# HGRN scores of a hybrid encoder layer: 128x128 score matmuls against two 64x64 matmuls on the halves of TensorE's columns

## The chip, the cores and the metric

The kernel runs on one core of a Trainium2 chip. The core has a matrix engine (TensorE, PE in the profile, with its weight loads shown apart as PEld), VectorE (DVE), ScalarE (ACT), GpSimd (POOL), SyncE (SP) and 16 DMA engines. TensorE reads both operands from SBUF and writes PSUM; ACT and DVE copy results out of PSUM. The metric is the device time of one execution in microseconds, the median over several runs.

## The reference

One encoder layer over 512 tokens of width 1024. Its first part mixes tokens in four HGRN heads and four mLSTM heads, each 128 wide; a cross-attention and a squared-ReLU MLP follow. The change touches the HGRN heads alone. Each head runs a gated scan forward and backward, and the two are summed:

```
S_t = diag(f_t) S_{t-1} + k_t v_t^T        (k_t = 1 - f_t)
o_t = S_t^T q_t
```

Written out, `o_t` is a sum over tokens `s` of a score times `v_s`, and the score is the sum over the 128 channels of `q_t k_s` times the product of the forget gates between `s` and `t`. That product depends on the channel, so scores can't be one plain matmul.

## The kernel before

Channels lie on the 128 partitions and the 512 tokens on the free axis. All large products are made of three fp32r matmuls (high by high, high by low, low by high: `mm3`, lines 225 to 227), each with 512 moving columns. For each 128x1024 piece of a weight matrix, ACT rounds it into `wh` (line 221) and DVE subtracts to get `wl` (line 222); a pair feeds 24 matmuls.

The HGRN scores are built by levels. For L = 1, 2, 4, ..., 64 the tokens are cut into blocks of 2L, and the scores between the two halves of such a block come from one product of `kc` (keys that are already multiplied by the gates up to the half's edge; made by `kcomb` on ACT, line 366) with the like-prepared queries `q2`. After each level `update` (DVE, lines 426, 429 and 433) multiplies queries, keys and gates by the next stretch of gates. Tokens are taken in four windows of 128, so a level is four fp32 matmuls of 128 keys by 128 tokens into one PSUM tile `sm` (line 376), and a predicated copy on DVE (line 381) takes from it the entries that belong to this level, by the mask `lm`, into the four diagonal blocks of the score matrix `A`. Ahead of the levels, line 361 makes the scores of a token with itself in the same way, and ACT copies them (line 362).

A fp32 matmul stands in the profile as two weight loads and two matmuls ("passes" below), so a score group of four matmuls has eight passes. A head's chain has one group of line 361 and seven of line 376; with four heads there are 32 groups.

The chain is a generator (`hgrn_chain`), and each `yield` gives way to the projections. Two heads are started at a time ("first pair", "second pair"). For the first pair, one step of a chain is taken after every 12 large matmuls; for the second (`rate[0] = 2`) two are taken, so that the groups of both heads stand together. The order on each engine is fixed when the program is built. On TensorE the instructions run in that order.

Of the kernel before, what the change touches and what calls it, by code (L numbers as in the profile page):

```python
# [13 lines left out]
AF = mybir.ActivationFunctionType  # L14
# [4 lines left out]
P = 128  # L19
# [58 lines left out]
def trunk(ctx: ExitStack, tc: tile.TileContext, x, mem, wpk, vec, cst, lmask, rmask, rows, out):  # L78
# [5 lines left out]
    v, sc, gp, pe = nc.vector, nc.scalar, nc.gpsimd, nc.tensor  # L84
    cnt = [0]

    def nm(s):
        cnt[0] += 1
        return f"{s}_{cnt[0]}"
# [7 lines left out]
    def smb():  # L97
        return pss.tile([P, 512], F32, tag="sm", name=nm("sm"))
# [4 lines left out]
    def ap(t, off, *dims):  # L103
        a = t[:, :]
        return bass.AP(a.tensor, a.offset + off, [list(a.ap[0])] + [list(d) for d in dims])
# [14 lines left out]
    lm = sb.tile([P, len(LEVELS) * P], U8, name="lm")  # L120
# [117 lines left out]
    def proj_d(mat, c0, xs, n=512, count=2):  # L238

        for j in range(count):  # L240
            wh, wl = weights(("d", mat, 0, c0 + P * j))
            ps = mmb()
            for k in range(8):
                z = slice(k * P, k * P + P)
                mm3(ps[:, :n], wh[:, z], wl[:, z], xs[k][0], xs[k][1], k == 0, k == 7)
                if k == 3:
                    tick()
            yield ps
            tick()
# [37 lines left out]
    for t in range(4):  # L287
# [4 lines left out]
        with tc.high_priority():  # L292
            for g in range(2):
                xg = xt[:, g * 512:g * 512 + 512]
                v.scalar_tensor_tensor(out=xg, in0=xg, scalar=r, in1=gmix[g], op0=ALU.mult, op1=ALU.mult)
                ps = smb()
# [51 lines left out]
    def hgrn_chain(h, s_):  # L348
        q, f, k = s_["q"], s_["f"], s_["k"]
        q2 = A4()  # L350
        v.tensor_tensor(out=q2[:, 0:512], in0=q[:, 0:512], in1=f[:, 512:1024], op=ALU.mult)
        v.tensor_tensor(out=q2[:, 512:1024], in0=q[:, 0:512], in1=f[:, 0:512], op=ALU.mult)
        A = A16()
        Adiag = ap(A, 0, [512 + P, 4], [1, P])
        kc = T2()
        v.tensor_tensor(out=kc[:, 0:512], in0=k[:, 0:512], in1=k[:, 512:1024], op=ALU.add)
        yield
        ps = smb()
        for w in range(4):
            z = slice(w * P, w * P + P)  # L360
            pe.matmul(ps[:, z], lhsT=kc[:, z], rhs=q[:, z], start=True, stop=True)
        sc.activation(Adiag, ps[:, :].rearrange("p (w t) -> p w t", t=P), AF.Copy)

        def kcomb(L):
            t = T2()
            sc.activation(t[:, 0:512].rearrange("p (b e j) -> p b e j", e=2, j=L),  # L366
                          ap(k, 0, [2 * L, 512 // (2 * L)], [512 + L, 2], [1, L]), AF.Copy)
            return t

        kc = kcomb(1)  # L370
        yield
        for li, L in enumerate(LEVELS):
            ps = smb()
            for w in range(4):
                z = slice(w * P, w * P + P)
                pe.matmul(ps[:, z], lhsT=kc[:, z],  # L376
                          rhs=ap(q2, w * P, [2 * L, P // (2 * L)], [512 + L, 2], [1, L]), start=True, stop=True)
            update(q2, k, f, L)
            if L < 64:
                kc = kcomb(2 * L)  # L380
            v.copy_predicated(Adiag, lm[:, li * P:li * P + P].unsqueeze(1).to_broadcast([P, 4, P]),
                              ps[:, :].rearrange("p (w t) -> p w t", t=P))
            yield

        ps = smb()
        for b in range(2):
            w0, w1 = slice(b * 256, b * 256 + P), slice(b * 256 + P, b * 256 + 256)
            pe.matmul(ps[:, b * 256 + P:b * 256 + 256], lhsT=k[:, w0], rhs=q2[:, 512 + b * 256 + P:512 + b * 256 + 256], start=True, stop=True)
            pe.matmul(ps[:, b * 256:b * 256 + P], lhsT=k[:, 512 + b * 256 + P:512 + b * 256 + 256], rhs=q2[:, w0], start=True, stop=True)

        sc.activation(ap(A, P, [1024 + 256, 2], [1, P]), ap(ps, P, [256, 2], [1, P]), AF.Copy)
        sc.activation(ap(A, 512, [1024 + 256, 2], [1, P]), ap(ps, 0, [256, 2], [1, P]), AF.Copy)
        update(q2, k, f, 128)
        yield

        for dr in range(2):
            ps = smb()
            for i in range(2):
                if dr == 0:
                    pe.matmul(ps[:, i * 256:i * 256 + 256], lhsT=k[:, i * P:i * P + P], rhs=q2[:, 768:1024], start=True, stop=True)  # L400
                else:
                    pe.matmul(ps[:, i * 256:i * 256 + 256], lhsT=k[:, 768 + i * P:768 + i * P + P], rhs=q2[:, 0:256], start=True, stop=True)
            dst = ap(A, 256, [512, 2], [1, 256]) if dr == 0 else ap(A, 1024, [512, 2], [1, 256])
            sc.activation(dst, ps[:, :].rearrange("p (i t) -> p i t", t=256), AF.Copy)
        yield
        ps = smb()
        for t in range(4):
            for s in range(4):
                pe.matmul(ps[:, t * P:t * P + P], lhsT=A[:, s * 512 + t * P:s * 512 + t * P + P],
                          rhs=vh[s][:, h * P:h * P + P], start=(s == 0), stop=(s == 3))  # L410
        o = T2()
        sc.activation(o[:, 0:512], ps, AF.Copy)
        yield
        yield from head_out(o, s_["gate"], V_HN + h, h)

    def update(q2, k, f, L):
        nb = 512 // (2 * L)
        if L == 128:
            qa, ta = ap(q2, 0, [896, 2], [1, P]), ap(f, 640, [-384, 2], [0, P])
            v.tensor_tensor(out=qa, in0=qa, in1=ta, op=ALU.mult)  # L420
            ka, tb = ap(k, 0, [896, 2], [1, P]), ap(f, 128, [640, 2], [0, P])
            v.tensor_tensor(out=ka, in0=ka, in1=tb, op=ALU.mult)
            return
        qa = ap(q2, 0, [512 + L, 2], [2 * L, nb], [1, L])
        ta = ap(f, 512 + L, [-(512 + L), 2], [2 * L, nb], [0, L])
        v.tensor_tensor(out=qa, in0=qa, in1=ta, op=ALU.mult)
        ka = ap(k, 0, [512 + L, 2], [2 * L, nb], [1, L])
        tb = ap(f, L, [512 - L, 2], [2 * L, nb], [0, L])
        v.tensor_tensor(out=ka, in0=ka, in1=tb, op=ALU.mult)
        if L < 128:  # L430
            fa = ap(f, 0, [512, 2], [2 * L, nb])
            fb = ap(f, L, [512, 2], [2 * L, nb])
            v.tensor_tensor(out=fa, in0=fa, in1=fb, op=ALU.mult)

    def head_out(o, gate, gcol, idx):

        junk = T2()
        ss = tiny(4)
        for t in range(4):
            z = slice(t * P, t * P + P)  # L440
            sc.activation(junk[:, z], o[:, z], AF.Square, accum_out=ss[:, t:t + 1])
        r, _ = rstd_of(ss, 4, P)
        v.tensor_tensor(out=o[:, 0:512].rearrange("p (t e) -> p t e", e=P),
                        in0=o[:, 0:512].rearrange("p (t e) -> p t e", e=P),
                        in1=r.unsqueeze(2).to_broadcast([P, 4, P]), op=ALU.mult)
        yield
        ps = smb()
        for t in range(4):
            z = slice(t * P, t * P + P)
            pe.transpose(ps[:, z], o[:, z], ident)  # L450
        v.scalar_tensor_tensor(out=gate, in0=ps, scalar=vc[:, gcol:gcol + 1], in1=gate, op0=ALU.mult, op1=ALU.mult)
        ys[idx] = hl(YT1())
        split_out(ys[idx][0], ys[idx][1], gate)
        yield
# [221 lines left out]
    def hgrn_start(p):  # L676
        for j in range(2):
            chains.append(hgrn_chain(2 * p + j, hst[2 * p + j]))
# [25 lines left out]
    for t in range(2):  # L704
        a = mt[t]
# [14 lines left out]
    for k in range(8):  # L720
        ps = smb()
# [226 lines left out]
    for f in range(4):  # L948

        sta = []  # L950
        for p in range(4):
            a = []
            for j in range(2):
                ps, = proj_d("up", 1024 * f + P * (p + 4 * j), x3, count=1)
# [57 lines left out]
        def ahead(n):  # L1012
            with tc.high_priority():
                for m in range(n, n + 3):
                    job(f, m)
            return job(f, n)

        n = 0
        while n < len(JOBS):
            p, g = JOBS[n]  # L1020
# [8 lines left out]
            w = ahead(n)  # L1029
# [96 lines left out]
```

## Time and profile before

| | before |
|---|---|
| median of 3 runs | 881.77 us (881.75 to 882.56) |
| profiled execution | 882.23 us, its span 880.4 us |
| PE busy, instructions | 855.4 us (97%), 4198 |
| DVE busy | 609.7 us (69%) |
| ACT busy | 415.2 us (47%) |
| granted TensorE clock | 1.00 in every stretch of the HGRN part |

A busy share says how long an engine had work under way. In the long views a group's row gives the engine, the operation, the tiles written and read, and the shapes; "128*128 128x512" means that the matmul uses all 128 rows and 128 columns of the array and writes 128 partitions by 512 columns. A merged row with "x8" gives the start of the first and the time to the end of the last.

### The profile page before, as it was taken

Reading aid. Unit: us, or ns where it says so; the run is one execution under the profiler, and the core shown is the slowest. Engines: PE = TensorE matmul, PEld = TensorE weight load, DVE = VectorE, ACT = ScalarE, POOL = GpSimd, SP = SyncE. Lnnn points to the kernel's source line nnn. Section 1 sums busy time; section 2 is a strip of 40 time slices with the busy share of each in tenths; the row PEclk is TensorE's granted clock in tenths of the full one; section 3 lists DMA queues with packets and bytes.
Section 4 is the critical chain, followed back from the end, with each engine's and each line's share of the span. In section 5 each row is a group of like instructions: output and inputs, shape, how many; then the busy total and the mean of one; then the engine's idle time right before and its main releaser. Section 6 shows DMA issues by size and latency. Waiting matters only on the chain.

```text
span 880.4 us, 11056 instructions
## 1 busy us (share of the span) xinstructions
PE 855.4 (97%) x4198; PEld 709.1 (81%) x4198; DVE 609.7 (69%) x1038; ACT 415.2 (47%) x758; POOL 19.2 (2%) x50
## 2 busy tenths in 40 slices
PE   7999999999999999999999999999999999999995
PEld 5887888888887897888888888878887888788874
DVE  5457688779446987644554456797678758866885
ACT  5235443363357667544544346543444445435544
POOL 2000000010010000000000000000000000000001
PEclk9999999999999999999999999999999999999998
DMA  6432222312132333432221422404330432142002
GB/s 259 135 102 73 72 73 72 120 60 65 58 119 72 97 100 116 144 120 96 72 73 48 168 85 83 144 1 143 120 120 1 167 120 96 33 171 108 25 1 96
DMA packets 24615, 84.21 MB, mean 96 GB/s; under 512 B 2865, under 2 KB 2993, under 8 KB 24562
## 3 DMA queue, kind: packets, MB, share of 16 engines
q1 hardware_dynamic: 24272, 83.04, 27.7%
q8 instruction: 33, 0.54, 0.3%
q10 hardware_dynamic: 290, 0.47, 0.2%
q14 instruction: 20, 0.16, 0.1%
HBM read 81.40 MB, written 2.10 MB: 95 GB/s over the span
## 4 chain that ended last, share of the span: by engine, by line
PE 65%; DVE 2%; ACT 1%; POOL 0%; issue 0%; POOLq 0%; ACTq 0%
PE mm L226 14%; PE mm L227 14%; PE mm L225 14%; PE sm L1008 5%; PE sm L1009 5%; PE sm L1010 5%; PE sm L629 2%; PE sm L614 2%; ACT wh L221 1%; PE mm L1010 1%; PE mm L1009 1%; PE mm L1008 1%; PE sm L768 1%; PE sm L227 1%; PE sm L226 1%; PE sm L225 1%
## 5 line engine op out<-in xcount | busy, mean ns | idle before, releaser
L225 PE MATMUL mm<-xT,wh 128*128 128x512 f32 x552 | 219.5, 399 | 0.0
L226 PE MATMUL mm<-xT,wh 128*128 128x512 f32 x552 | 216.2, 392 | 0.2 <-DVE xT L774 0.2
L227 PE MATMUL mm<-xT,wl 128*128 128x512 f32 x552 | 216.1, 391 | 0.0
L222 DVE TENSOR_TENSOR wl<-st,wh 128x1024 fp32r<-128x1024 f32 x109 | 133.3, 1223 | 109.9 <-ACT wh L221 106.5
L221 ACT ACTIVATE wh<-st 128x1024 fp32r<-128x1024 f32 x109 | 115.4, 1059 | 183.7 <-PE mm L226 86.7
L227 PEld LDWEIGHTS mm<-xT,wl 128*128 128x128 f32 x552 | 103.6, 188 | 22.1 <-issue 0.6
L225 PEld LDWEIGHTS mm<-xT,wh 128*128 128x128 f32 x552 | 103.8, 188 | 21.5 <-issue 1.4
L226 PEld LDWEIGHTS mm<-xT,wh 128*128 128x128 f32 x552 | 103.8, 188 | 21.3 <-DVE xT L774 0.9
L1008 PE MATMUL sm<-wh,yT 128*128 128x512 f32 x128 | 49.9, 397 | 4.8 <-ACT wh L221 4.8
L227 PE MATMUL mm<-wh,yT 128*128 128x512 f32 x128 | 50.6, 395 | 0.0
L225 PE MATMUL mm<-wh,yT 128*128 128x512 f32 x128 | 50.4, 394 | 0.0
L226 PE MATMUL mm<-wl,yT 128*128 128x512 f32 x128 | 50.1, 391 | 0.0
L1009 PE MATMUL sm<-wl,yT 128*128 128x512 f32 x128 | 49.9, 390 | 0.0
L1010 PE MATMUL sm<-wh,yT 128*128 128x512 f32 x128 | 49.2, 389 | 0.0
L964 DVE SCALAR_TENSOR_TENSOR t<-mm,rg 128x512 f32<-128x512 f32 x32 | 22.1, 690 | 38.3 <-PE mm L227 38.3
L221 ACT ACTIVATE wh<-as 128x1024 fp32r<-128x1024 f32 x24 | 25.4, 1058 | 35.0 <-PE sm L1010 17.9
L935 DVE TENSOR_TENSOR vv<-sm,vv 128x512 f32<-128x512 f32 x48 | 31.9, 684 | 4.8 <-PE sm L1010 4.7
L1008 PEld LDWEIGHTS sm<-wh,yT 128*128 128x128 f32 x128 | 23.7, 188 | 12.6 <-ACT wh L221 6.5
L221 ACT ACTIVATE wh<-a 128x1024 fp32r<-128x1024 f32 x20 | 21.2, 1062 | 24.3 <-PE sm L1010 21.8
L222 DVE TENSOR_TENSOR wl<-a,wh 128x1024 fp32r<-128x1024 f32 x20 | 24.4, 1222 | 11.1 <-ACT wh L221 11.1
L376 PEld LDWEIGHTS sm<-a,t 128*128 128x128 f32 x224 | 30.1, 191 | 2.2 <-ACT t L366 0.4
L222 DVE TENSOR_TENSOR wl<-as,wh 128x1024 fp32r<-128x1024 f32 x24 | 29.4, 1223 | 3.2 <-ACT wh L221 3.0
(265 smaller groups left out, 1574.7 us busy)
## 6 DMA issues: line engine op xcount, KB each, us to landing
st<-in_wpk SPq DMA_DIRECT2D x109, 512.0 KB, 3.3
as<-in_wpk SPq DMA_DIRECT2D x16, 512.0 KB, 4.1
gate<-in_wpk SPq DMA_DIRECT2D x8, 512.0 KB, 4.3
a<-in_wpk SPq DMA_DIRECT2D x8, 512.0 KB, 4.9
as<-in_x SPq DMA_DIRECT2D x4, 512.0 KB, 6.4
vv<-in_x SPq DMA_DIRECT2D x8, 256.0 KB, 4.4
out<-vv SPq DMA_DIRECT2D x7, 256.0 KB, 2.2
a<-in_mem SPq DMA_DIRECT2D x2, 512.0 KB, 3.9
```

Of the source, the lines that this page charges most:

```text
L221: sc.activation(dst_hi, src, AF.Copy)
L222: v.tensor_tensor(out=dst_lo, in0=src, in1=dst_hi.bitcast(F32), op=ALU.subtract)
L225: pe.matmul(ps, lhsT=ah, rhs=bh, start=first, stop=False)
L226: pe.matmul(ps, lhsT=ah, rhs=bl, start=False, stop=False)
L227: pe.matmul(ps, lhsT=al, rhs=bh, start=False, stop=last)
L376: pe.matmul(ps[:, z], lhsT=kc[:, z], rhs=ap(q2, w * P, [2 * L, P // (2 * L)], [512 + L, 2], [1, L]), start=True, stop=True)
L614: pe.matmul(ps, lhsT=k[:, ws * P:ws * P + P], rhs=q, start=True, stop=True)
L935: v.tensor_tensor(out=z, in0=ps, in1=z, op=ALU.add)
L964: v.scalar_tensor_tensor(out=y, in0=ps, scalar=0.0, in1=rrow[:, 0:512], op0=ALU.max, op1=ALU.mult)
L1008: pe.matmul(ps, lhsT=ah, rhs=bh, start=new, stop=False, **fl)
L1009: pe.matmul(ps, lhsT=ah, rhs=bl, start=False, stop=False, **fl)
L1010: pe.matmul(ps, lhsT=al, rhs=bh, start=False, stop=end and k == 1, **fl)
```

## The change

Each score matmul of 128 keys by 128 tokens becomes two of 64 keys by 64 tokens: keys 0 to 63 of a window go to the array's columns 0 to 63 and so to PSUM partitions 0 to 63, keys 64 to 127 to the other half. For L < 64 both halves take the tokens of their own half window (pairs across the half windows have no entry at those levels); for L = 64 each takes the tokens of the other one. What is copied out is then a 64x64 square for each window in each half of the partitions, so there are two copies of 64 partitions by 256 elements where there was one of 128 by 512. At L = 64 the squares hold only entries of that level, and ACT copies them without a mask.

```diff
+        def half(t, step, j, i):
+            a = t[64 * j:64 * j + 64, :]
+            return bass.AP(a.tensor, a.offset + 64 * i, [list(a.ap[0]), [step, 4], [1, 64]])
...
         for w in range(4):
-            z = slice(w * P, w * P + P)
-            pe.matmul(ps[:, z], lhsT=kc[:, z], rhs=q[:, z], start=True, stop=True)
-        sc.activation(Adiag, ps[:, :].rearrange("p (w t) -> p w t", t=P), AF.Copy)
+            for j in range(2):
+                z = slice(w * P + 64 * j, w * P + 64 * j + 64)
+                pe.matmul(ps[64 * j:64 * j + 64, z], lhsT=kc[:, z], rhs=q[:, z], start=True, stop=True)
+        for j in range(2):
+            sc.activation(half(A, 512 + P, j, j), half(ps, P, j, j), AF.Copy)
...
             for w in range(4):
-                z = slice(w * P, w * P + P)
-                pe.matmul(ps[:, z], lhsT=kc[:, z],
-                          rhs=ap(q2, w * P, [2 * L, P // (2 * L)], [512 + L, 2], [1, L]), start=True, stop=True)
+                for j in range(2):
+                    ks = kc[:, w * P + 64 * j:w * P + 64 * j + 64]
+                    if L == 64:
+                        i = 1 - j
+                        rhs = q2[:, w * P + i * 576:w * P + i * 576 + 64]
+                    else:
+                        i = j
+                        rhs = ap(q2, w * P + 64 * i, [2 * L, 64 // (2 * L)], [512 + L, 2], [1, L])
+                    pe.matmul(ps[64 * j:64 * j + 64, w * P + 64 * i:w * P + 64 * i + 64], lhsT=ks, rhs=rhs, start=True, stop=True)
             update(q2, k, f, L)
...
-            v.copy_predicated(Adiag, lm[:, li * P:li * P + P].unsqueeze(1).to_broadcast([P, 4, P]),
-                              ps[:, :].rearrange("p (w t) -> p w t", t=P))
+            for j in range(2):
+                if L == 64:
+                    sc.activation(half(A, 512 + P, j, 1 - j), half(ps, P, j, 1 - j), AF.Copy)
+                else:
+                    v.copy_predicated(half(A, 512 + P, j, j), lm[64 * j:64 * j + 64, li * P + 64 * j:li * P + 64 * j + 64].unsqueeze(1).to_broadcast([64, 4, 64]),
+                                      half(ps, P, j, j))
```

In the first pair the order on TensorE stays as it was but for the groups themselves. At the second block of the first pair there stands before (`sm` is the PSUM tile of scores, `t` the keys and queries, `mm` the accumulator of a projection):

```order
L226 MATMUL mm_725<-xT_86,wh_638 128x512
L227 MATMUL mm_725<-xT_86,wl_639 128x512
L361 MATMUL sm_760<-t_83_478,t_120_717 128x128 x4
L225 MATMUL mm_774<-xT_85,wh_674 128x512
L226 MATMUL mm_774<-xT_85,wh_674 128x512
```

and after the change:

```order
L226 MATMUL mm_725<-xT_86,wh_638 128x512
L227 MATMUL mm_725<-xT_86,wl_639 128x512
L367 MATMUL sm_765<-t_83_478,t_120_717 64x64 x8
L225 MATMUL mm_784<-xT_85,wh_674 128x512
L226 MATMUL mm_784<-xT_85,wh_674 128x512
```

Four matmuls have become eight in the same place. In the second pair the groups move. Before, TensorE has the two heads' groups of a level (L = 4) side by side, in one block, with 12 large matmuls ahead of it:

```order
L226 MATMUL mm_1516<-wl_1435,xT_85 128x512
L227 MATMUL mm_1516<-wh_1434,xT_85 128x512
L376 MATMUL sm_1611<-a_244_1485,t_267_1579 128x128 x4
L376 MATMUL sm_1622<-a_247_1491,t_269_1590 128x128 x4
L225 MATMUL mm_1517<-wh_1434,xT_85 128x512
L226 MATMUL mm_1517<-wl_1435,xT_85 128x512
```

After the change the same two groups stand seven large matmuls apart:

```order
L391 MATMUL sm_1721<-a_244_1565,t_267_1683 64x64 x8
L226 MATMUL mm_1607<-wl_1515,xT_85 128x512
L227 MATMUL mm_1607<-wh_1514,xT_85 128x512
L225 MATMUL mm_1607<-wh_1514,xT_85 128x512
L226 MATMUL mm_1607<-wl_1515,xT_85 128x512
L227 MATMUL mm_1607<-wh_1514,xT_85 128x512
L225 MATMUL mm_1608<-wh_1514,xT_85 128x512
L226 MATMUL mm_1608<-wl_1515,xT_85 128x512
L391 MATMUL sm_1737<-a_247_1571,t_269_1699 64x64 x8
```

Counted over the second pair, the 16 groups stood in 10 blocks with 86 large matmuls between the first block and the last, and now stand in 11 blocks with 96 between them. In the first pair there are 16 blocks before and after. DVE's order in the second pair (`a` are queries, keys and gates, `as` is `A`), at L = 4, is before:

```order
L426 TENSOR_TENSOR a_244_1485<-a_244_1485,a_155_924 128x2x64x4
L429 TENSOR_TENSOR a_156_925<-a_156_925,a_155_924 128x2x64x4
L381 COPY_PREDICATED as_1488<-lm,sm_1611 128x4x128
L433 TENSOR_TENSOR a_155_924<-a_155_924 128x128
L426 TENSOR_TENSOR a_247_1491<-a_247_1491,a_165_983 128x2x64x4
```

and after (lines 426, 429 and 433 have become 444, 447 and 451):

```order
L444 TENSOR_TENSOR a_244_1565<-a_244_1565,a_155_959 128x2x64x4
L447 TENSOR_TENSOR a_156_960<-a_156_960,a_155_959 128x2x64x4
L399 COPY_PREDICATED as_1568<-lm,sm_1721 64x4x64
L451 TENSOR_TENSOR a_155_959<-a_155_959 128x128
L399 COPY_PREDICATED as_1568<-lm,sm_1721 64x4x64
L444 TENSOR_TENSOR a_247_1571<-a_247_1571,a_165_1028 128x2x64x4
```

The copy stands there in two halves around the update of the gates. The orders of GpSimd and of the DMA queue are the same.

## Rows read from the trace of the kernel before

**Rows 1.** The page: span, busy time by engine, the chain's shares by engine.

```profile
span 880.4 us, 11056 instructions
...
PE 855.4 (97%) x4198; PEld 709.1 (81%) x4198; DVE 609.7 (69%) x1038; ACT 415.2 (47%) x758; POOL 19.2 (2%) x50
...
PE 65%; DVE 2%; ACT 1%; POOL 0%; issue 0%; POOLq 0%; ACTq 0%
```

**Rows 2.** Busy time by stretches of the HGRN part (clock, DMA share last).

```profile
core 0: us, PE busy (x) PEld busy (x) DVE busy (x) ACT busy (x) POOL busy (x), PEclk, DMA share, GB/s
...
100.00:120.00 20.00, 20.00 (x111) 17.49 (x110) 17.19 (x28) 8.91 (x13) 0.00 (x0) 1.00 0.24 78
...
186.00:198.00 12.00, 12.00 (x74) 10.95 (x74) 11.34 (x18) 7.95 (x12) 0.00 (x0) 1.00 0.20 66
198.00:210.00 12.00, 12.00 (x72) 10.49 (x71) 12.00 (x21) 3.37 (x6) 0.00 (x0) 1.00 0.16 48
210.00:222.00 12.00, 12.00 (x77) 10.53 (x76) 12.00 (x24) 4.00 (x6) 0.00 (x0) 1.00 0.27 87
```

**Rows 3.** PE in order of time: a score block at L = 8, first pair.

```profile
114.91 0.39 PE L227 MATMUL mm<-xT,wl 128*128 128x512 f32 x1
115.13 1.05 PE L376 MATMUL sm<-a,t 128*128 128x128 f32 x8
115.94 0.48 PE L225 MATMUL mm<-xT,wh 128*128 128x512 f32 x1
116.26 0.40 PE L226 MATMUL mm<-xT,wh 128*128 128x512 f32 x1
116.49 0.39 PE L227 MATMUL mm<-xT,wl 128*128 128x512 f32 x1
```

**Rows 4.** The same at L = 1 and L = 2, first pair.

```profile
95.94 1.49 PE L376 MATMUL sm<-a,t 128*128 128x128 f32 x8
97.13 0.54 PE L225 MATMUL mm<-xT,wh 128*128 128x512 f32 x1
97.51 0.39 PE L226 MATMUL mm<-xT,wh 128*128 128x512 f32 x1
...
104.07 1.13 PE L376 MATMUL sm<-a,t 128*128 128x128 f32 x8
104.94 0.49 PE L225 MATMUL mm<-xT,wh 128*128 128x512 f32 x1
105.28 0.40 PE L226 MATMUL mm<-xT,wh 128*128 128x512 f32 x1
```

**Rows 5.** The same for a block of two groups, second pair.

```profile
201.00 1.95 PE L376 MATMUL sm<-a,t 128*128 128x128 f32 x16
202.70 0.48 PE L225 MATMUL mm<-wh,xT 128*128 128x512 f32 x1
203.02 0.39 PE L226 MATMUL mm<-wl,xT 128*128 128x512 f32 x1
```

**Rows 6.** PE around matmuls that use 64 of the array's rows (64*128).

```profile
275.45 0.39 PE L227 MATMUL mm<-xT,wl 128*128 128x512 f32 x1
275.77 0.50 PE L599 MATMUL sm<-ar,selr 64*128 64x512 f32 x1
276.11 0.39 PE L600 MATMUL sm<-ar,selr 64*128 64x512 f32 x1
276.42 0.50 PE L225 MATMUL mm<-xT,wh 128*128 128x512 f32 x1
276.76 0.40 PE L226 MATMUL mm<-xT,wh 128*128 128x512 f32 x1
276.99 0.40 PE L227 MATMUL mm<-xT,wl 128*128 128x512 f32 x1
```

**Rows 7.** PE and PEld: matmuls of 32 and (transposes, after a wait) 64 moving columns.

```profile
57.13 1.20 PE L500 MATMUL sm<-tiny,a 128*128 128x32 f32 x10
58.16 0.48 PE L225 MATMUL mm<-xT,wh 128*128 128x512 f32 x1
...
69.58 0.43 PE L554 MATMUL sm<-cs,a 64*128 64x64 f32 x4 [1.67 <-DVE a L543]
...
69.55 0.32 PEld L554 LDWEIGHTS sm<-cs,a 64*128 64x128 f32 x4 [2.06 <-issue]
...
L554 PEld LDWEIGHTS sm<-cs,a x4: 134/138/140, 69.6 to 69.7; 64*128 64x128 f32 x4
```

**Rows 8.** All of line 376 on PE: ns min/median/max, first and last start.

```profile
L376 PEld LDWEIGHTS sm<-a,t x224: 186/192/197, 95.7 to 221.6; 128*128 128x128 f32 x112
L376 PE MATMUL sm<-a,t x224: 270/275/378, 95.9 to 221.7; 128*128 128x128 f32 x112
L376 PEldq EVENT_SEMAPHORE  x21: 51/51/51, 92.6 to 216.9; - x21
```

**Rows 9.** DVE in order of time, second pair.

```profile
205.01 0.67 DVE L429 TENSOR_TENSOR a<-a,a 128x512 f32<-128x512 f32 x1
205.62 0.72 DVE L381 COPY_PREDICATED as<-lm,sm 128x512 f32<-128x512 uint8 x1
206.25 0.37 DVE L433 TENSOR_TENSOR a<-a 128x128 f32<-128x128 f32 x1
```

**Rows 10.** Groups by line and shape: busy us, mean ns.

```profile
L381 DVE COPY_PREDICATED as<-lm,sm 128x512 f32<-128x512 uint8 x28 | 20.4, 728 | 0.0
L727 DVE SCALAR_TENSOR_TENSOR a<-sm,vc,a 128x256 fp32r<-128x256 f32 x8 | 3.3, 478 | 0.9 <-ACT a L726 0.9
L331 DVE SCALAR_TENSOR_TENSOR t<-mm,vc,t 128x512 f32<-128x512 f32 x4 | 3.0, 745 | 0.0
L222 DVE TENSOR_TENSOR wl<-st,wh 128x1024 fp32r<-128x1024 f32 x109 | 133.3, 1223 | 109.9 <-ACT wh L221 106.5 <-PE sm L376 3.3
L362 ACT ACTIVATE as<-sm 128x512 f32<-128x512 f32 x4 | 2.3, 590 | 2.2 <-PE sm L361 2.2
L391 ACT ACTIVATE as<-sm 128x256 f32<-128x256 f32 x4 | 1.5, 376 | 3.8 <-PE sm L389 3.8
```

**Rows 11.** Waits of 186 to 222 us: us in total, times, longest.

```profile
ACT t L366 <- DVE a L429: 13.9, 6, 5.0
...
PEld sm L376 <- ACT t L366: 0.4, 1, 0.4
```

More of the change, by code (lines that the diff above doesn't have):

```diff
@@ L353, in hgrn_chain @@
         A = A16()
-        Adiag = ap(A, 0, [512 + P, 4], [1, P])
+        def half(t, step, j, i):
+            a = t[64 * j:64 * j + 64, :]
+            return bass.AP(a.tensor, a.offset + 64 * i, [list(a.ap[0]), [step, 4], [1, 64]])
         kc = T2()
```

## The prediction

> **What bounds the kernel now.** I read the page first. PE is busy 97% of the span, and the chain that ended last is PE for 65% with DVE at 2% and ACT at 1% [rows 1]. So time that TensorE saves or loses counts one for one wherever nothing else is as full. Next I read the stretches of the HGRN part [rows 2], because an average over the span hides them. In the first pair of heads (100 to 120 us) DVE is busy 17.2 of 20 us, so it has some room. In the second pair (186 to 222 us) PE and DVE are both full: DVE 11.3 of 12, then 12.0 of 12 twice. There the two engines bound the kernel together, and a gain on PE alone is cut off by DVE. ACT has room in all of them. The clock reads 1.00 throughout, so all PE durations compare directly.
>
> Then I read PE in order of time, and took starts to starts, since PE's ends are modelled. Large matmuls start 0.23 us apart (116.26 to 116.49 in [rows 3]). A group of eight passes delays the second large matmul behind it to 1.13 us after its own start (115.13 to 116.26), of which 0.23 is the first large one; so a group costs 0.90 us, 0.111 to 0.112 a pass. Measuring to the second one is necessary, as the first starts early and runs long.
>
> **What the score groups cost now.** At L = 1 a group costs 1.57 - 0.23 = 1.34 us and at L = 2 it costs 1.21 - 0.23 = 0.98 us [rows 4]; the moving operand is read there in runs of one or two elements. Two groups in one block cost 2.02 - 0.23 = 1.79 us [rows 5], twice 0.90, so blocks have no price of their own. I take 0.90 for line 361 and all levels from 4 up. A pair of heads has 16 groups: 12 x 0.90 + 2 x 1.34 + 2 x 0.98 = 15.4 us, and both pairs 30.9 us of PE time. That is all the change can touch on PE.
>
> **What it adds: changes of the array's shape.** The new matmuls use 64 of the array's columns, and the matmuls around them use all 128. The trace has no 128*64 matmul, but it has 64*128 ones. From 275.45 to 276.99 us there are five starts to starts, which would take 1.15 us at 0.23; they take 1.54 [rows 6]. Going into the other shape and back therefore costs 0.39 us: the matmul ahead of a change and the one behind it each hold the next by about 0.1 us more. With 16 blocks in the first pair that is 6.2 us, and with 11 in the second 4.3 us, 10.5 us in all. The bound below: on the way in only 64 columns of weights must be loaded uncovered and not 128. If half of one 0.11 is saved so, 27 changes cost 1.5 us less.
>
> **What a pass costs then.** Eight passes of 128 by 128 become 16 of 64 by 64, eight for each half of the columns. This is the disputed price, and its bounds are far apart.
> - One pass after the other, each at half of 0.111: 0.056 us. The row nearest to it by shape is the 64-column transposes, whose weight loads start (0.32 - 0.138)/3 = 0.061 us apart [rows 7]. A pass with 32 moving columns and 128 of weights still takes 1.03/10 = 0.103 us [rows 7]; so here the loading of weights sets the pace, and it must halve with the columns too.
> - Both halves at once: half of that, 0.028 us.
> - Weights no longer loaded behind the running matmul: 0.056 + 0.056 = 0.112 us.
>
> I take 0.028. The halves hold different weights, write different partitions, and follow each other as two passes here, two there, so that the second pass of one can run beside the first of the other. No row shows this; what speaks for it is that the array does load weights while it streams (PEld and PE of line 376 overlap, [rows 8]), so the parts that a second stream needs are not all taken. The 0.061 row stands behind a wait of 1.67 us that had emptied the queue, so it may be the rate at which instructions arrive. Before line 376 PE's instruction queue runs 3.1 us ahead (the wait instruction is done at 92.6, the first load starts at 95.7 [rows 8]), longer than a group takes.
>
> [...]
>
> **The sum.** A group takes 16 x 0.028 = 0.45 us. L = 1 and L = 2 keep their extra cost for short runs: 2 x 0.44 + 2 x 0.08 = 1.04 us a pair, half of it (0.5) with both halves at once.
> - First pair: 16 x 0.45 + 0.5 + 6.2 = 13.9 us against 15.4: a gain of 1.5 us. DVE has room here.
> - Second pair: 16 x 0.45 + 0.5 + 4.3 = 12.0 us against 15.4: 3.4 us less PE work. But DVE is full. Its copies start 0.63 us before the next instruction (205.62 to 206.25, [rows 9]); half as many elements cost 745 - 478 = 267 ns less on DVE reading PSUM [rows 10], so 0.36 us. 14 copies x 0.63 = 8.8 us become 24 x 0.36 = 8.6 us, since L = 64 goes to ACT. DVE's stretch stays as long, less 0.2 us. What can still be won is that 96 large matmuls instead of 86 run inside it: 10 x 0.23 = 2.3 us of PE work that is no longer to be done later, less 10/24 of one more weight split of 1.22 us [rows 10] (0.5 us). That makes 1.9 to 2.0 us; I take 1.9.
>
> Nothing else is charged. ACT gets 16 copies of 0.38 us where it had four of 0.59 [rows 10], 3.7 us more over some 140 us, in stretches where it is busy at most 8 of 12 us. The copy in two pieces frees a PSUM tile one DVE instruction later (0.37 us, line 433 in [rows 9]); what it could delay is a group two steps on, and in the second pair groups waited only 0.4 us in all [rows 11].
>
> 882.23 - 1.5 - 1.9 = 878.8 us. This is made against the profiled execution, which is 0.46 us above the median of the runs; I forecast 878.6 us, about 0.36% less than before.
>
> **The rivals.**
> - **One half after the other** (the change does not do what it says). A group costs 16 x 0.056 = 0.90 us as before, and the shape changes are pure loss: 32 x 0.90 + 2.1 + 10.5 - 30.9 = +10.5 us, 892.5 us. At 0.061 us, or if the instruction queue is the limit, +13.1 us, 895.3 us. For it: no row shows two matmuls at once, and the only short row reads 0.061. It decides from 0.038 us a pass on: there 512 passes, 10.5 us for changes and about 1 us for short runs make up the 30.9 us. 32 in 100.
> - **Partly at once**, say 0.042 us a pass, because loads of one half hold those of the other: 512 x 0.042 + 1.4 + 10.5 - 30.9 = +2.5 us, 884.7 us. 12 in 100.
> - **DVE takes the second pair's gain.** The halves run at once, but the chains wait on DVE and ACT at the new places: ACT's `kcomb` already waits 13.9 us for DVE there [rows 11]. Only the first pair's 1.5 us or less is left, 880.3 to 882 us. 10 in 100.
> - **Weights uncovered**, 0.112 us a pass: 512 x 0.112 + 2.1 + 10.5 - 30.9 = +39 us, 921 us. Against it: in [rows 6] lines 599 and 600, both in the other shape, start 0.34 us apart, no more than 0.23 and the 0.1 of the change itself, so the second load was covered. 5 in 100.
>
> **How the numbers follow.** My forecast has 41 in 100, and lies between 876.5 us (changes 1.5 us cheaper, some more from the second pair) and 880.0 us (0.030 us a pass). About 0.2%, 1.8 us, is what a measurement of this kernel can tell from no change. The forecast's case is faster (0.41). The DVE rival and the cheap end of the partial one are the same (0.13). The rest is slower (0.46). The range that holds 8 in 10 must reach from the forecast's low end over the serial case at 0.056: 876.5 to 893.5 us. It leaves out the dearer serial end and the uncovered weights. The likeliest case's own range is 876.5 to 880.0.
>
> **What the profile after would show.** If I am right, 16 passes of a group start about 0.03 us apart on average, pairwise close together, and a block at L = 8 takes 0.84 us to the second large matmul less 0.23. [...] The large matmuls ahead of and behind a block should each hold the next by 0.1 us more; if not, the shape changes are free and the gain is larger. DVE copies should read about 0.46 us and start 0.36 us before their successor; in the second pair DVE should stay full and PE should begin to wait for it. The prediction is wrong above all if the halves don't overlap.

## The result and the profile after

The changed kernel takes 885.17 us (median of 5 runs, 884.93 to 886.71) against 881.78 us for the kernel before in the same session (5 runs, 881.75 to 883.34). The ratio is 1.0039, 95% interval 1.0024 to 1.0053: slower by 3.4 us, where 3.2 us less (878.6 us against 881.77) had been forecast. Lines move: the score matmuls are lines 367 and 391 now, ACT's copies 369 and 397, the predicated copy 399, `kcomb` 373, and `update` 444, 447 and 451 (426, 429 and 433 before).

The page after, as in [rows 1]:

```profile
span 884.6 us, 11595 instructions
...
PE 853.2 (96%) x4454; PEld 696.2 (79%) x4454; DVE 613.9 (69%) x1058; ACT 419.5 (47%) x770; POOL 19.2 (2%) x50
...
PEclk9999999999899999999999999999999999999998
```

PE is busy 2.2 us less in a span that is 4.2 us longer, and the eleventh of the 40 slices has a lower clock, which it had not before. The page says no more than that PE now stands still somewhere. A score block at L = 8 in the first pair, in order of time on PE and PEld, and all of line 391 (ns min/median/max), as in [rows 3] and [rows 8]:

```profile
114.54 0.39 PE L227 MATMUL mm<-xT,wl 128*128 128x512 f32 x1
114.86 0.69 PE L391 MATMUL sm<-a,t 128*64 128x64 f32 x16
115.47 0.50 PE L225 MATMUL mm<-xT,wh 128*128 128x512 f32 x1
115.81 0.39 PE L226 MATMUL mm<-xT,wh 128*128 128x512 f32 x1
...
114.86 0.55 PEld L391 LDWEIGHTS sm<-a,t 128*64 128x64 f32 x16 [0.35 <-issue]
...
L391 PE MATMUL sm<-a,t x448: 222/222/369, 96.6 to 226.4; 128*64 128x64 f32 x150
```

One pass lasts 222 ns, and 16 passes end 0.69 us after the first began, so they start (0.69 - 0.22) / 15 = 0.031 us apart. The average hides pairs: in this block the trace has one pass of each half start 0.007 us apart, and the next pair mostly 0.05 us later. From the large matmul ahead of the block to the second one behind it are 1.27 us; in [rows 3] they are 1.35. So on PE the block is 0.08 us shorter (0.06 was forecast).

Where the time went shows when large matmuls (lines 225 to 227) are counted in both traces and the starts of the same number are compared. About 0.7 us of difference is there from the first large matmuls on, ahead of the HGRN part:

| start before, us | start after, us | after minus before |
|---|---|---|
| 82.32 | 83.02 | +0.70 |
| 149.67 | 148.62 | -1.05 |
| 183.46 | 182.41 | -1.05 |
| 209.31 | 206.57 | -2.73 |
| 222.26 | 216.80 | -5.46 |
| 234.67 | 239.10 | +4.43 |
| 315.68 | 320.11 | +4.43 |

The first pair gives 1.75 us. In the second pair PE runs further ahead, and everything and more is lost between 217 and 239 us. Busy time by stretches of the second pair after, as in [rows 2], then finer around the loss:

```profile
core 0: us, PE busy (x) PEld busy (x) DVE busy (x) ACT busy (x) POOL busy (x), PEclk, DMA share, GB/s
186.00:198.00 12.00, 11.21 (x119) 8.81 (x114) 10.86 (x18) 7.69 (x13) 0.00 (x0) 1.00 0.21 68
198.00:210.00 12.00, 11.49 (x101) 8.44 (x100) 11.71 (x23) 3.48 (x5) 0.00 (x0) 1.00 0.26 81
210.00:222.00 12.00, 10.36 (x95) 7.43 (x94) 11.69 (x24) 5.16 (x7) 0.00 (x0) 1.00 0.14 53
222.00:250.00 28.00, 25.11 (x160) 22.03 (x160) 12.13 (x25) 9.50 (x19) 0.00 (x0) 0.88 0.12 39
...
220.00:222.00 2.00, 0.39 (x14) 0.25 (x10) 1.97 (x4) 1.39 (x2) 0.00 (x0) 1.00 0.00 0
222.00:224.00 2.00, 0.69 (x16) 0.55 (x16) 1.96 (x5) 0.76 (x3) 0.00 (x0) 0.93 0.27 47
224.00:226.00 2.00, 0.43 (x8) 0.43 (x10) 1.91 (x6) 0.63 (x1) 0.00 (x0) 0.50 0.59 223
226.00:228.00 2.00, 2.00 (x17) 1.67 (x14) 2.00 (x4) 0.76 (x2) 0.00 (x0) 0.50 0.00 0
228.00:230.00 2.00, 2.00 (x6) 1.54 (x5) 2.00 (x5) 0.00 (x0) 0.00 (x0) 0.50 0.00 0
```

PE was busy in all of these 64 us before; the last 28 of them, which [rows 2] does not show, read before:

```profile
222.00:250.00 28.00, 28.00 (x166) 24.75 (x165) 9.90 (x18) 10.63 (x28) 0.22 (x1) 1.00 0.21 65
```

Now PE is idle for 64 - 58.17 = 5.8 us. DVE is nearly as full as it was (in 198 to 222 us 11.7 of 12 us, 12.0 before). PE works 0.39 of the 2 us from 220 us on and 0.69 of the next 2; towards the end of these the granted clock falls to 0.50, and it is still there while PE is full again (226 to 230 us). PE after in order of time:

```profile
219.28 0.40 PE L227 MATMUL mm<-wh,xT 128*128 128x512 f32 x1
219.70 0.69 PE L391 MATMUL sm<-a,t 128*64 128x64 f32 x16
222.06 0.69 PE L391 MATMUL sm<-a,t 128*64 128x64 f32 x16 [1.67 <-ACT t L373]
225.57 1.12 PE L391 MATMUL sm<-a,t 128*64 128x64 f32 x16 [2.83 <-ACT t L373]
226.63 0.80 PE L225 MATMUL mm<-xT,wh 128*128 128x512 f32 x1
227.22 0.63 PE L226 MATMUL mm<-xT,wh 128*128 128x512 f32 x1
227.65 0.63 PE L227 MATMUL mm<-xT,wl 128*128 128x512 f32 x1
```

Three groups (of 16 passes each) stand here with no large matmul between them. The last two wait for `kcomb` (line 373), which waits for DVE's update. Large matmuls then start 0.43 us apart instead of 0.23 until 230.21. DVE after, in the same stretch:

```profile
215.93 0.68 DVE L447 TENSOR_TENSOR a<-a,a 128x512 f32<-128x512 f32 x1
216.65 0.44 DVE L399 COPY_PREDICATED as<-lm,sm 64x256 f32<-64x256 uint8 x1
216.99 0.21 DVE L451 TENSOR_TENSOR a<-a 128x32 f32<-128x32 f32 x1
217.21 0.45 DVE L399 COPY_PREDICATED as<-lm,sm 64x256 f32<-64x256 uint8 x1
217.69 0.69 DVE L444 TENSOR_TENSOR a<-a,a 128x512 f32<-128x512 f32 x1
...
225.85 1.29 DVE L585 TENSOR_TENSOR vv<-mm,t 128x512 f32<-128x512 f32 x2
```

The copies are shorter, but their neighbours stand further apart than in [rows 9]: the large update starts 0.72 us ahead of the first piece (0.61 before), and the second piece 0.48 us ahead of the next update (0.36 was forecast). And the two copies of line 585 have to do with PE's missing work: they take a finished projection out of PSUM, so that its accumulators come free for the next one. In DVE's order they stand behind the score copies, so in PE's order, which is fixed when the program is built, the next large matmuls stand behind the three groups. The first follows at 226.63, 0.78 us after these copies begin.

### The profile page after: what moved, and what is told of

Same layout as the page of the kernel before. It is cut to its first block, busy times and chain, and to the rows that moved or that the text cites. A ratio compares the mean times of both kernels' runs of the same rounds, so it can differ in the third digit from the quotient of the medians.

```text
span 884.6 us, 11595 instructions
## 1 busy us (share of the span) xinstructions
PE 853.2 (96%) x4454; PEld 696.2 (79%) x4454; DVE 613.9 (69%) x1058; ACT 419.5 (47%) x770; POOL 19.2 (2%) x50
## 4 chain that ended last, share of the span: by engine, by line
PE 65%; DVE 2%; ACT 1%; POOL 0%; issue 0%; POOLq 0%; ACTq 0%
PE mm L226 14%; PE mm L227 14%; PE mm L225 14%; PE sm L1026 5%; PE sm L1028 5%; PE sm L1027 5%; PE sm L647 2%; PE sm L632 2%; ACT wh L221 1%; PE mm L1028 1%; PE mm L1027 1%; PE mm L1026 1%; PE sm L786 1%; PE sm L227 1%; PE sm L226 1%; PE sm L225 1%
## 5 line engine op out<-in xcount | busy, mean ns | idle before, releaser
L373 ACT ACTIVATE t<-a 128x512 f32<-128x512 f32 x28 | 18.3, 672 | 24.7 <-DVE a L447 15.1
```

## The experiments

The theory from here on: (1) the halves do run at once, and PE gains what was forecast; (2) a copy that starts at partition 64 makes DVE's neighbours wait, so DVE's chain in the second pair grows; (3) PE, now faster, runs out of large matmuls, waits for that chain, and loses clock on top. The rivals are named with the runs. Each run's median stands against the kernel before in the same session: 881.96 us for the runs with halves in one pair, with early copies in the change and with one copy, 882.06 us for the other four. "DVE's stretch" is the time from the last sum of keys to the first L = 128 update of the second pair, read from the starts; it was 41.55 us before and is 46.09 us after.

**Halves in the first pair only.**

```diff
+    HALVES = lambda h: h < 2
...
-        for w in range(4):
-            for j in range(2):
+        if HALVES(h):
+            for w in range(4):
+                for j in range(2):
...
+        else:
+            for w in range(4):
+                z = slice(w * P, w * P + P)
+                pe.matmul(ps[:, z], lhsT=kc[:, z], rhs=q[:, z], start=True, stop=True)
```

> Halves for the first two heads alone, the other two as before. My theory now (the halves win on TensorE everywhere, and the loss is a wait for VectorE at the end of the second pair): faster than before by the 1.75 us that the large matmuls of the first pair came earlier in the trace of the change, 880.0 us. Rival (the halves or their changes of the array's shape cost time wherever they stand): half of the 3.4 us lost, 883.5 us.

Measured: 880.38 us, ratio 0.998 (0.9971 to 0.9989). By starts of large matmuls the first pair gives 1.76 us, and nothing is lost later. So part 1 of the theory holds there, where DVE has room, and the rival (883.5 us) is out.

**Halves in the second pair only.** The same edit with `h >= 2`.

> Halves for the last two heads alone. My theory: all of the loss and none of the first pair's gain, 885.2 + 1.75 = 886.9 us, with TensorE waiting for the second pair's last groups (1.7 and 2.8 us) and the clock at 0.5 behind them. Rival (cost spread over all groups): 883.5 us.

Measured: 887.69 us, ratio 1.0059 (1.0046 to 1.0071). PE is idle 5.8 us of 186 to 250 us and the clock in 222 to 250 us is 0.88, both as in the whole change. The time is 0.8 us above the 886.9 us expected and far from the rival's 883.5. The two parts add up to 5.7 - 1.6 = 4.1 us, near the whole change's 3.4.

**The next projection's copies ahead of the score copies.** The change, with a higher priority for what is line 585:

```diff
-            v.tensor_tensor(out=ap(d, 0, [129, 4], [1, P]), in0=ps[:, :].rearrange("p (h e) -> p h e", e=P),
-                            in1=b[:, 0:512].rearrange("p (h e) -> p h e", e=P), op=ALU.add)
+            with tc.high_priority():
+                v.tensor_tensor(out=ap(d, 0, [129, 4], [1, P]), in0=ps[:, :].rearrange("p (h e) -> p h e", e=P),
+                                in1=b[:, 0:512].rearrange("p (h e) -> p h e", e=P), op=ALU.add)
```

> The change, with VectorE's copies of the mLSTM value projection (which free TensorE's four accumulators) put ahead of the score copies in the planned order. My theory: TensorE had nothing to run beside the last three score groups because the accumulators were still held; now 16, 18, 6 and 9 large matmuls stand between the last groups, the waits of 1.7 and 2.8 us and the slow clock go, and the time is 877 to 880 us. Rival (VectorE's longer work in the second pair sets the time whatever the order): 884 us or more.

Measured: 879.17 us, ratio 0.9964 (0.9951 to 0.9976), 6.0 us under the change. Busy time by stretches of this run:

```profile
210.00:222.00 12.00, 12.00 (x91) 9.24 (x90) 11.77 (x23) 3.95 (x6) 0.00 (x0) 1.00 0.16 51
222.00:250.00 28.00, 27.97 (x202) 24.09 (x202) 12.95 (x28) 13.88 (x37) 1.91 (x2) 1.00 0.28 91
```

From 210 us on PE is full and the clock 1.00, while DVE's stretch is still 46.7 us long; from 186 to 210 us PE is idle for 1.3 us, as in the change. So most of the loss goes when PE has large matmuls to do while the long chain runs, and the time, 2.8 us under the kernel before, falls in the forecast's own range.

**The same early copies in the kernel before.** The same edit, nothing else.

> The kernel before with VectorE's copies of the next projection out of PSUM put ahead of the score copies, and nothing else. Theory: TensorE was busy in all of 222 to 250 us before, so the early copies release nothing that was waited for: 881.0 to 882.8 us; what the same edit gave the changed kernel (885.17 to 879.17) was a loss of the change taken back. Rival (the edit gains by itself, whatever the matmuls are): 877 to 880 us.

Measured: 882.06 us, ratio 1.0 (0.9991 to 1.0008), and PE busy 28.00 of 28 us as before. The early copies gain nothing by themselves. In the change they take its loss back, and what PE's shorter blocks save then shows.

**Two pieces of columns, none from partition 64.** The matmuls of before; the predicated copy of a level in two pieces of 64 columns of each window on all 128 partitions; L = 64 copied by ACT as in the change.

```diff
-            v.copy_predicated(Adiag, lm[:, li * P:li * P + P].unsqueeze(1).to_broadcast([P, 4, P]),
-                              ps[:, :].rearrange("p (w t) -> p w t", t=P))
+            for j in range(2):
+                if L == 64:
+                    sc.activation(half(A, 512 + P, j, 1 - j), half(ps, P, j, 1 - j), AF.Copy)
+                else:
+                    v.copy_predicated(ap(A, 64 * j, [512 + P, 4], [1, 64]), lm[:, li * P + 64 * j:li * P + 64 * j + 64].unsqueeze(1).to_broadcast([P, 4, 64]),
+                                      ap(ps, 64 * j, [P, 4], [1, 64]))
```

> The kernel before, with its full 128-column score matmuls, and each level's copy out of PSUM as two pieces of 64 columns of every window on all 128 partitions (256 elements a partition, as in the change; level 64 by two ScalarE copies, as in the change). Theory (a piece that starts at partition 64 makes VectorE's neighbours wait): no piece starts at partition 64 here, so start to start a piece takes 0.33 to 0.36 us, and from the large update ahead of a piece to that piece 0.60 us as before; VectorE's stretch from the last sum of keys to the first L=128 update of the second pair stays at 41.0 to 42.5 us (before 41.55); time 881 to 884 us. Rival (two pieces instead of one are what costs, wherever they start): pieces 0.40 us and 0.70 us behind the update, as in the changed kernel, the stretch 44 to 46 us and the time above 885 us, and the same as in the run with pieces of 64 partitions.

Its result stands beside that of the next run.

**Two pieces of 64 partitions, as in the change.** The run before this one with the pieces `half(A, 512 + P, j, j)` of the change in their place. Both pieces have 256 elements a partition, as there, and the order of instructions on every engine and the semaphores that DVE waits for are the same as in that run.

> The same kernel and the same order of instructions on each engine as the run with column pieces, but the pieces of the VectorE copies are those of the change: 64 partitions each, the second from partition 64, 256 elements a partition. Theory (the start at partition 64): update to piece 0.72 us, piece to the gate update 0.34 us, gate update to the second piece 0.22 us, piece to the next update 0.45 to 0.48 us, as in the changed kernel; VectorE's stretch of the second pair 2 to 3 us longer than with column pieces (43.5 to 45.5 us), and the time 1.5 to 8 us over that run, more than 3 if TensorE runs dry and its clock falls. Rival (two pieces cost the same wherever they start): the stretch and the time within 0.5 us and 1 us of the run with column pieces.

Measured: with pieces of columns 882.78 us, ratio 1.0005 (0.9996 to 1.0014); with pieces of partitions 884.74 us, ratio 1.003 (1.0019 to 1.004). DVE's stretch is 42.35 us in the one and 44.90 us in the other. PE is never idle from 186 to 250 us in the one, and 0.9 us in the other, with the clock at 1.00 in both. DVE in order of time, pieces of columns:

```profile
212.61 0.70 DVE L439 TENSOR_TENSOR a<-a,a 128x512 f32<-128x512 f32 x1
213.21 0.46 DVE L391 COPY_PREDICATED as<-lm,sm 128x256 f32<-128x256 uint8 x1
213.54 0.23 DVE L443 TENSOR_TENSOR a<-a 128x32 f32<-128x32 f32 x1
213.67 0.46 DVE L391 COPY_PREDICATED as<-lm,sm 128x256 f32<-128x256 uint8 x1
214.00 0.69 DVE L436 TENSOR_TENSOR a<-a,a 128x512 f32<-128x512 f32 x1
```

The same with pieces of partitions:

```profile
212.50 0.68 DVE L439 TENSOR_TENSOR a<-a,a 128x512 f32<-128x512 f32 x1
213.22 0.44 DVE L391 COPY_PREDICATED as<-lm,sm 64x256 f32<-64x256 uint8 x1
213.57 0.25 DVE L443 TENSOR_TENSOR a<-a 128x64 f32<-128x64 f32 x1
213.83 0.45 DVE L391 COPY_PREDICATED as<-lm,sm 64x256 f32<-64x256 uint8 x1
214.31 0.69 DVE L436 TENSOR_TENSOR a<-a,a 128x512 f32<-128x512 f32 x1
```

Ahead of the first piece 0.72 us against 0.60, behind the second 0.48 against 0.33 (the gate updates between the pieces are of different levels here; at equal levels they show 0.10 more ahead of the second piece). Only behind the first piece nothing is added (0.35 and 0.33). In the column run each instruction starts before the one ahead of it has ended; in the other the two pieces, and what follows the second, start 0.01 to 0.04 us after that. The first piece begins at partition 0, but the piece that DVE copied last before it began at 64. The pieces differ in a second thing, 64 partitions for 128, and the first level of the same run (pieces of partitions) tells which of the two it is:

```profile
192.12 0.69 DVE L436 TENSOR_TENSOR a<-a,a 128x512 f32<-128x512 f32 x1
192.73 0.43 DVE L391 COPY_PREDICATED as<-lm,sm 64x256 f32<-64x256 uint8 x1
...
194.23 0.69 DVE L436 TENSOR_TENSOR a<-a,a 128x512 f32<-128x512 f32 x1
194.95 0.44 DVE L391 COPY_PREDICATED as<-lm,sm 64x256 f32<-64x256 uint8 x1
```

Both pieces begin at partition 0 and have 64 partitions. The one at 192.73 is the first score copy of its pair, and what DVE read from PSUM last before it began at partition 0: it starts 0.61 us behind its update. The other follows a piece from partition 64 and starts 0.72 us behind. Part 2 of the theory holds: the place of the start costs, not the number of pieces nor their partitions. The kernel with the old matmuls is slower by 2.0 us for it (2.7 us between the profiled executions, whose spans are 882.5 and 879.8 us).

**Both halves into the same columns, one copy.** The change, but both halves write the same 256 columns of `ps`, each in its own half of the partitions. One copy of 128 partitions by 256 then takes a level into a compact tile, and ACT moves the result into `A` after L = 32. (The scores of a token with itself go into the compact tile too, and the mask is laid out to match.) The edit does two things at once: it halves the number of DVE's copies, and none starts at partition 64.

```diff
+        C = A[:, 2048:2304]
...
-                    pe.matmul(ps[64 * j:64 * j + 64, w * P + 64 * i:w * P + 64 * i + 64], lhsT=ks, rhs=rhs, start=True, stop=True)
+                    pe.matmul(ps[64 * j:64 * j + 64, w * 64:w * 64 + 64], lhsT=ks, rhs=rhs, start=True, stop=True)
...
+                v.copy_predicated(C.rearrange("p (w t) -> p w t", t=64), lm[:, li * P:li * P + 64].unsqueeze(1).to_broadcast([P, 4, 64]),
+                                  ps[:, 0:256].rearrange("p (w t) -> p w t", t=64))
+            if L == 32:
+                for j in range(2):
+                    sc.activation(half(A, 512 + P, j, j), half(A, 64, j, 0, 2048), AF.Copy)
```

> The change, with the results of both halves written into the same 256 columns of PSUM and gathered in a compact 128 by 256 square by one predicated copy a level (and two ScalarE copies into the score matrix after level 32). VectorE's score copies go from 48 of 64 partitions to 24 of 128. My theory: copies that start on partition 64 make VectorE's neighbours wait (0.12 us on either side); here a copy should start 0.36 us before its successor and the update before it 0.60 us before it, the second pair's stretch on VectorE shrinks by 4 us or more, and the time is 876 to 880 us. Rival (VectorE's share does not matter, the order of the groups does): about 885 us.

Measured: 877.68 us, ratio 0.9947 (0.9934 to 0.9959), 4.3 us under the kernel before. DVE's stretch is 38.38 us. Its DVE in order of time, and its busy time by stretches:

```profile
205.06 0.70 DVE L450 TENSOR_TENSOR a<-a,a 128x512 f32<-128x512 f32 x1
205.66 0.45 DVE L399 COPY_PREDICATED as<-lm,sm 128x256 f32<-128x256 uint8 x1
205.99 0.28 DVE L454 TENSOR_TENSOR a<-a 128x64 f32<-128x64 f32 x1
...
210.00:222.00 12.00, 12.00 (x107) 9.12 (x107) 10.53 (x21) 6.96 (x14) 0.00 (x0) 1.00 0.14 45
222.00:250.00 28.00, 28.00 (x162) 24.68 (x161) 7.36 (x14) 11.27 (x32) 2.02 (x2) 1.00 0.30 94
```

**Both remedies together.** The compact copy and the early copies of line 585.

> The matmuls of the change with both halves written to the same 256 columns of PSUM and one 128 by 256 copy a level, and VectorE's copies of the next projection out of PSUM put ahead of the score copies. Theory: the first of the two alone already left TensorE busy for all of the stretch from 186 to 250 us, so that nothing is left for the second to give: 876.5 to 878.5 us, the same as without it (877.68). Rival (the late projection still cost something there, hidden in full busy digits): 875 us or less.

Measured: 877.51 us, ratio 0.9949 (0.9936 to 0.9961), the same as the compact copy alone. With PE full (busy 63.98 of the 64 us from 186 to 250 us with the compact copy alone) there is nothing left for the second remedy to give.

## Why the prediction was wrong

- **A pass at 0.028 us: right.** The halves run at once; 0.031 us was measured. The 0.061 row was no limit: at that pace the starts of 16 passes would span 15 x 0.061 = 0.92 us, and those of line 391 span 0.47.
- **Changes of shape at 0.39 us: right.** The step into the block takes 0.32 us and the one behind it 0.34, each about 0.1 over 0.23, and the 0.61 us of the block are 0.14 over the 0.47 within which the passes start: 0.34 us in all.
- **The first pair's gain of 1.5 us: right.** 1.75 us by starts, 1.6 us in the run with that part alone.
- **"DVE's stretch stays as long, less 0.2 us": the step that failed first.** The copies themselves were sized well: 0.33 us for 128 partitions by 256 elements, 0.34 us for the first piece of the change. What the sum left out is the wait that a start at another partition puts between neighbours: about 0.12 us ahead of the first piece, 0.10 ahead of the second and 0.15 behind it, some 0.37 us a level, for the 12 levels that DVE copies in this pair up to 4.4 us. The stretch grew by 4.5 us (46.09 against 41.55): about these 4.4 us, 0.9 us more in DVE's waits of over 0.1 us, and 0.5 us because two pieces take 0.66 us where one copy took 0.62, less 1.2 us for the two copies of L = 64 that went to ACT. In the run with pieces of partitions the waits of 0.37 us a level add 2.5 us to the stretch and not 4.4, in part since the run with column pieces has 1.4 us more of those longer waits. The trace after shows where: the first piece started 0.72 us behind an update of 0.69 us when DVE's last read of PSUM ahead of it had begun at partition 64, and 0.61 us behind an update of 0.68 us when that read had begun at partition 0 too (the first score copy of the second pair); the update behind the piece from partition 64 started 0.48 us behind a piece of 0.45 us; the gate update behind the piece from partition 0 started 0.34 us behind a piece of 0.44 us, before its end. What in DVE causes these waits was not shown.
- **"Nothing else is charged", since groups waited only 0.4 us: the second.** That was a wait of the old PE. The prediction said that PE would begin to wait for DVE, and put no price on it. A faster PE, against a chain that did not get shorter, had to wait, and the large matmuls that would have filled the wait were held up by DVE's copies of line 585. By estimate the waits and the lower clock together cost about 7.9 us: 5.8 us idle, and 4.4 us of work at a clock of 0.50 in 224 to 230 us, of which (0.43 - 0.23) / 0.43, 2.1 us, would not have been needed at 1.00. Against the 3.4 us that PE's shorter blocks were to save, that leaves a loss of 4.5 us; by starts the second pair lost 4.43 + 1.05 = 5.5 us. The estimate is low in part because a large matmul's record lasts 0.39 us where the next starts after 0.23, so that the first part of each wait counts as busy.
- **The rivals.** "DVE takes the second pair's gain" named the place and the engine, but it ended at the gain lost and had no row for a loss. The measured time lies close to that of "partly at once" (884.7 us), and that is chance: its mechanism did not occur. It also lies within the wide range of 876.5 to 893.5 us, but that reached so far up for the serial rival's sake, whose mechanism did not occur either.
- **Slips in the sums.** 882.23 - 1.5 - 1.9 - 0.46 is 878.4, not 878.6, and at 0.061 us a pass the serial rival comes to +12.9 us, not +13.1. Neither changes the argument.

How the loss divides among the waits around the copies, the missing large matmuls and the clock is not settled: they depend on each other, and either of two edits takes all of it back. The change's matmuls in its own order of instructions, but without the waits around the copies, were not tried.

## What to carry to other kernels

Where two engines are full together, a gain on one must be followed into the other with the price of each pair of neighbours, start to start, and not only with the durations. A result that is spread over both halves of the partitions is worth laying out so that one copy from partition 0 takes it; here that, with half as many copies, turned a loss of 3.4 us into a gain of 4.3. And an engine that is made faster needs other work at hand for the waits it now meets: look at what frees the buffers of that work, and at the clock behind a wait.

## What the hardware showed that was not expected

- Two matmuls of 64 by 64 on the two halves of the columns overlapped almost wholly: 16 passes of 222 ns began within 0.47 us, the two of a pair 0.007 us apart. This was forecast, but no row before had shown it.
- In the run with pieces of partitions, DVE's copy from partition 64 started 0.01 us after the instruction ahead had ended, and the update behind it and the next score copy, though that begins at partition 0, 0.03 to 0.04 us after: start to start 0.48 against 0.33 us behind it and 0.72 against 0.60 ahead of the next, for the same number of elements a partition.
- Behind a wait of 1.67 us, and within the next one of 2.83 us, the granted clock went from 1.00 to 0.50, and large matmuls then started 0.43 us apart instead of 0.23 for 3.6 us of work.
